# The start of a decoder-layer kernel: conditioning row by transposes, more modulation buffers, `u` ahead of the weight copies

## The chip, the cores and the metric

One core of a Trainium2 chip runs the whole program. The metric is the device time of one execution in microseconds (us). Matrix work is done by TensorE (PE), element-wise work by VectorE (DVE) and ScalarE (ACT); GpSimd (POOL) only sets constants here. SyncE (SP) issues every DMA, in program order, on one queue.

## What is computed

The reference is one residual decoder layer on 256 tokens of width 2048. Each of its two halves is modulated by a conditioning vector `c`:

```python
c_act = jax.nn.silu(c)
mod = c_act @ w_mod[l] + b_mod[l]
sh1, sc1, g1, sh2, sc2, g2 = jnp.split(mod[:, None, :], N_MOD, axis=-1)
u = x * (1.0 + sc1) + sh1
y = token_mixer(u, w_in[l], ...)
x = layer_norm(DEEPNORM_ALPHA * x + (1.0 + g1) * y, ln1_g[l], ln1_b[l])
u = x * (1.0 + sc2) + sh2
y = swiglu(u, w_gate[l], w_up[l], w_down[l])
x = layer_norm(DEEPNORM_ALPHA * x + (1.0 + g2) * y, ln2_g[l], ln2_b[l])
```

The token mixer begins with a large product `u @ w_in` whose columns feed an mLSTM group (`qk`, `v`, `o`) and an HGRN2 group (`f`, `q`, `i`, `g`). HGRN2 has a lower bound `lb` from a softmax over layers; with one layer it is zero, but the kernel still computes it.

## The kernel before

The token axis (256) lies along the free dimension, the width 2048 is cut into 16 rows of 128 partitions, called k = 0 to 15. All weights come from HBM as float32. Each 128x1024 weight tile is split into a high part (`wh`, an ACT copy to fp32r) and a low part (`wl`, a DVE subtraction, L214), and each product is three matmuls: high weight by high `u` (L250), high weight by low `u` (L251), low weight by high `u` (L252).

**Modulation.** `mod(j)` (L172) makes 128 of the 6 x 2048 modulation values: it loads a 1024 KB tile `m` of the transposed `w_mod` (L174) and DVE multiplies it with `cb` and sums along the row (L175), giving one column of `modc`. `cb` holds silu(c) in all 128 partitions. The tiles `m` have two buffers. At the start `cb` is filled by one DMA that reads the 8 KB vector `c` 128 times (L141), and two ACT passes then apply silu to it in place. A second, column-wise copy of silu(c), `ca`, is made from the packed constants `pk` (L143).

**Row k of `u`.** `make_u(k)` (L270) needs columns 16+k (scale) and k (shift) of `modc` and the transposed `x`, which comes in four loads of 512 KB (L274), one for four rows. ACT computes `u`, ACT copies it to the high part `uh`, and DVE subtracts to get the low part `ul` (L232). `prep(n)` calls `mod(16+k)`, `mod(k)` and `make_u(k)` for the rows below n.

**Order of the input product.** `STAGES` lists sections. The first is `fq`, rows 0 to 3: `fq_part` (L325) holds eight PSUM banks and for each row first runs `prep(k + 1)`, then loads two weight tiles (L209) and runs 48 matmuls on them. So every row of this section needs 2 MB of modulation weights and 1 MB of weights. After it come `qk`, `g`, `i`, `v` on rows 0 to 3 (first group), the same on rows 4 to 7 (second group), `fq` on rows 4 to 15 and the rest; the other 12 rows of `u` are prepared while these run. `evac` adds up sections; the tiles `q`, `f`, `i`, `g`, `qk`, `v` and the four halves of `uh`, `ul` take all ten buffers of the pool `big`, from which `A()` allocates.

**Order on the engines.** A scheduler orders the instructions; `tc.high_priority` raises those inside it, and the weight copies (`wh`, `wl`) have it with `PRI["w"]`. Each engine then works through its list in order: an instruction that waits holds up all behind it. `lower_bound()` (L303) is called when the first section's work is done; its first operation depends on `pk` alone. The constants `kc` (identity, two masks) and `mk` are loaded in row 3 of the first section (L330, L332).

Of the kernel before, what the change touches and what calls it, by code (L numbers as in the profile page):

```python
# [3 lines left out]
F32 = mybir.dt.float32  # L4
F32R = mybir.dt.float32r
U8 = mybir.dt.uint8
AF = mybir.ActivationFunctionType
ALU = mybir.AluOpType

P = 128  # L10
T = 256
# [69 lines left out]
def build(nc, tc, d):  # L81
    from contextlib import ExitStack

    with ExitStack() as ctx:
# [41 lines left out]
        def act(out, in_, f, **kw):  # L126
            if f in sets:
                use_set(f)
            i = nc.scalar.activation(out, in_, f, **kw).ins  # L129
            if f in sets:  # L130
                tc.add_manual_dep(i, table["load"].name, order, reason="table")
                table["used"].append(i)
            return i
# [4 lines left out]
        mm = nc.tensor.matmul  # L138

        cb = cst.tile([P, D], F32, name="cb")  # L140
        nc.sync.dma_start(cb, d["c"].broadcast_to([P, D]))  # L141
        pk = cst.tile([P, NPK], F32, name="pk")
        nc.sync.dma_start(pk, d["pk"])  # L143
        kc = cst.tile([P, NCST], F32, name="kc")
        kr = cst.tile([P, 256], F32R, name="kr")
        mk = cst.tile([P, NMK], U8, name="mk")

        def pc(n, i=0, w=1):
            return pk[:, PK[n][0] + i : PK[n][0] + i + w]
# [8 lines left out]
        one = cst.tile([P, P], F32, name="one1")  # L158
        nc.gpsimd.memset(one, 1.0)

        for i in range(2):
            o = cb[:, 1024 * i : 1024 * i + 1024]
            act(o, o, AF.Silu)
        init = cst.tile([P, 96], F32, name="init")
        nc.vector.tensor_copy(init, pc("bmod", 0, 96))
        for s in (1, 2, 4, 5):
            ts(init[:, 16 * s : 16 * s + 16], pc("bmod", 16 * s, 16), 1.0, None, ALU.add)
        ca = cst.tile([P, 16], F32, name="ca")
        act(ca, pc("c", 0, 16), AF.Silu)
        modc = cst.tile([P, 96], F32, name="modc")  # L170

        def mod(j):  # L172
            t = mr.tile([P, D], F32, tag="m", name=f"m{j}")
            nc.sync.dma_start(t, d["wmod"][j])  # L174
            table["mod"] = nc.vector.tensor_tensor_reduce(t, t, cb, 1.0, init[:, j : j + 1], ALU.mult, ALU.add, modc[:, j : j + 1]).ins  # L175
            yield
# [24 lines left out]
        def col(s, k):  # L201
            return modc[:, 16 * s + k : 16 * s + k + 1]
# [27 lines left out]
        def split(hi, lo, src):  # L230
            act(hi, src, AF.Copy)
            tt(lo, src, hi.bitcast(F32), ALU.subtract)  # L232

        def pair(n):
            return [A(F32R, name=f"{n}h{i}") for i in range(2)], [A(F32R, name=f"{n}l{i}") for i in range(2)]

        def kt(tiles, k):
            if len(tiles) > 2:
                return tiles[k]
            t = tiles[k // 8]  # L240
            return t[:, (k % 8) * T : (k % 8) * T + T]
# [21 lines left out]
                    mm(o, b, h[:, w], start=False, stop=last and k == nk - 1, skip_group_check=True)  # L263


        uh, ul = pair("u")

        xt = {}

        def make_u(k):  # L270
            u = S(T, "t", bufs=CFG["t"])
            if k % 4 == 0:
                xt["t"] = M(name="xT")
                nc.sync.dma_start(xt["t"], d["x"][k // 4])  # L274
            act(u, xt["t"][:, (k % 4) * T : (k % 4) * T + T], AF.Identity, scale=col(1, k), bias=col(0, k))
            split(kt(uh, k), kt(ul, k), u)

        acc = {"q": A(name="q"), "f": A(name="f"), "i": A(name="i"), "g": A(name="g"), "qk": A(name="qk"), "v": A(name="v")}

# [22 lines left out]

        def lower_bound():  # L303
            e, pr = lbt[:, 0:8], lbt[:, 8:16]
            tt(e, pc("lb", 0, 8), pc("lb", 0, 8), ALU.subtract)
            act(e, e, AF.Exp)
            nc.vector.reciprocal(pr, e)
            tt(pr, pr, e, ALU.mult)
            tt(lb, pr, pr, ALU.subtract)
            ts(oml, lb, -1.0, 1.0, ALU.mult, ALU.add)  # L310
# [14 lines left out]
        def fq_part(k0, k1):  # L325
            banks = [ps() for _ in range(8)]
            for k in range(k0, k1):
                prep(k + 1)
                if k == 3:
                    nc.sync.dma_start(kc, d["kc"])  # L330
                    mf = M(NMK, name="mf")
                    nc.sync.dma_start(mf, d["mk"])  # L332
                    nc.vector.tensor_copy(mk, mf)
                    act(kr[:, 0:P], ident, AF.Copy)
                    act(kr[:, P:], kc[:, 192:320], AF.Copy)
                for c, (h, l) in enumerate(next_win()):
                    gB(banks[4 * c : 4 * c + 4], h, l, 1, 1024, uh, ul, k, k == k0, k == k1 - 1)
                    yield
            if k1 == KT:
                next(ga)  # L340
            for i in range(8):
                evac(k0, "fq", i, banks[i])
# [67 lines left out]
        for st in head:  # L410
            gen = part(*st)
            unit = work([st]) / (2 * (st[3] - st[2]) if st[0] == "fq" else (st[3] - st[2]) // 2)
            for _ in gen:
                done += unit
                if done > start:
                    prep(min(KT, head[0][3] + (KT - head[0][3]) * (done - start) / (total - start)))
            if done == start:
                lower_bound()


# [640 lines left out]
def lay(x, c, w_mod, b_mod, w_in, conv_w, conv_b, b_igate, b_fgate, mlstm_norm_w, hgrn_norm_w, lb_logits, w_out, ln1_g, ln1_b, w_gate, w_up, w_down, ln2_g, ln2_b):  # L1061
# [10 lines left out]

    wm, wi, wo, wg, wu, wd = w_mod[0], w_in[0], w_out[0], w_gate[0], w_up[0], w_down[0]
    a = {}
    a["c"] = c.reshape(1, D)
    a["wmod"] = np.ascontiguousarray(wm.T).reshape(96, P, D)
    a["wmk"] = np.concatenate([wm[:, s * D : s * D + D].reshape(KT, P, D) for s in PE_SECT] or [wm[:1, :1].reshape(1, 1, 1)])
    a["x"] = x[0].T.reshape(4, 4, P, T).transpose(0, 2, 1, 3).reshape(4, P, 1024)
# [45 lines left out]
```

## Time and profile before

| what | before |
|---|---|
| median of 3 runs | 1257.38 us (1256.13 to 1259.53) |
| the profiled execution, own time | 1258.37 us |
| its span (first to last instruction) | 1256.3 us |
| PE busy | 1210.4 us, 96% of the span |
| DVE busy | 906.4 us, 72% |
| ACT busy | 595.0 us, 47% |
| DMA, 16 engines | 328 MB, mean 261 GB/s |

The profiled execution is 2.1 us longer than its span and 1.0 us longer than the median of the runs. The page shares busy time over the whole span; the first 50 us of 1256 are one slice and a half of its forty, so the change has to be read in windows and in the timeline of the first 60 us. "Matmul" rows give the time of one instruction through the pipeline; how fast PE works is the distance from one start to the next.

### The profile page before, as it was taken

The numbers are of one execution on the slowest core, as the hardware profiler recorded it, in microseconds if no ns is written. First come the engines' busy times: TensorE is split into PE (matmuls) and PEld (weight loads), VectorE is DVE, ScalarE is ACT, GpSimd is POOL, SyncE is SP. The second block draws the span as 40 slices with busy tenths as digits, with TensorE's granted clock in tenths as the row PEclk, the third lists the DMA queues.
The fourth block names the chain that finished last, engine by engine and source line by source line (L and its number), as shares of the span: only waits on it lengthen the run. The fifth ranks groups of instructions, "written<-read, shape, count | busy, mean of one in ns | idle before, by whom it ended". The sixth has DMA issues, their size and how long they took to land.

```text
span 1256.3 us, 17142 instructions
## 1 busy us (share of the span) xinstructions
PE 1210.4 (96%) x6706; PEld 1038.6 (83%) x6706; DVE 906.4 (72%) x987; ACT 595.0 (47%) x751; POOL 3.9 (0%) x13
## 2 busy tenths in 40 slices
PE   4799999999999999899999999999999999999996
PEld 4789899997889888788888888888888888888885
DVE  6688987999999867979688895555555445445665
ACT  3554445745565643664444444434344444444340
POOL 0000000000000000000000000000000000000000
PEclk9899999999999999999999999999999999999998
DMA  9998998856888896689898886566666666676661
GB/s 361 358 337 337 335 388 314 309 202 235 297 314 310 312 330 229 228 329 373 276 336 328 316 289 198 173 198 189 197 191 191 192 188 187 193 255 186 196 201 67
DMA packets 75968, 328.00 MB, mean 261 GB/s; under 512 B 8432, under 2 KB 8816, under 8 KB 62704
## 3 DMA queue, kind: packets, MB, share of 16 engines
q1 hardware_dynamic: 75888, 326.92, 74.9%
q8 instruction: 52, 0.85, 0.3%
q14 instruction: 28, 0.23, 0.0%
HBM read 324.79 MB, written 2.10 MB: 260 GB/s over the span
## 4 chain that ended last, share of the span: by engine, by line
PE 90%; DVE 4%; ACT 3%; DMA 1%; issue 1%; DVEq 0%; ACTq 0%
PE ps L726 21%; PE ps L725 21%; PE ps L729 21%; PE ps L250 5%; PE ps L252 5%; PE ps L251 5%; PE ps L261 2%; PE ps L262 2%; PE ps L263 2%; DVE m L175 1%; PE ps L448 1%; DMA m<-in_wmod 1%; ACT wh L129 1%; DVE wl L214 1%; PE ps L881 1%
## 5 line engine op out<-in xcount | busy, mean ns | idle before, releaser
L129 ACT ACTIVATE wh<-wr 128x1024 fp32r<-128x1024 f32 x405 | 427.8, 1059 | 535.4 <-PE ps L726 389.1
L719 DVE TENSOR_TENSOR wl<-wr,wh 128x1024 fp32r<-128x1024 f32 x293 | 356.5, 1223 | 258.6 <-ACT wh L129 254.2
L725 PE MATMUL ps<-wh,u2h 128*128 128x512 f32 x704 | 274.6, 391 | 3.2 <-ACT u2h L129 3.2
L726 PE MATMUL ps<-wh,u2l 128*128 128x512 f32 x704 | 274.5, 391 | 0.0
L175 DVE CUSTOM_DVE_ANT_0 m<-m,cb,init 128x2048 f32<-128x2048 f32 x96 | 225.0, 2346 | 21.5 <-DMA m<-in_wmod 21.3
L729 PE MATMUL ps<-wl,u2h 128*128 128x512 f32 x704 | 217.3, 390 | 0.0
L250 PE MATMUL ps<-uh,wh 128*128 128x256 f32 x640 | 184.9, 294 | 24.1 <-ACT wh L129 16.9
L251 PE MATMUL ps<-ul,wh 128*128 128x256 f32 x640 | 182.2, 287 | 0.0
L252 PE MATMUL ps<-uh,wl 128*128 128x256 f32 x640 | 180.5, 287 | 1.1 <-DVE wl L214 1.0
L725 PEld LDWEIGHTS ps<-wh,u2h 128*128 128x128 f32 x704 | 132.2, 188 | 31.0 <-ACT u2h L129 3.6
L726 PEld LDWEIGHTS ps<-wh,u2l 128*128 128x128 f32 x704 | 132.6, 189 | 27.9 <-DVE u2l L849 0.7
L729 PEld LDWEIGHTS ps<-wl,u2h 128*128 128x128 f32 x704 | 132.5, 188 | 27.6
L214 DVE TENSOR_TENSOR wl<-wr,wh 128x1024 fp32r<-128x1024 f32 x112 | 135.8, 1221 | 24.2 <-ACT wh L129 23.5
L250 PEld LDWEIGHTS ps<-uh,wh 128*128 128x128 f32 x640 | 124.1, 195 | 26.4 <-ACT wh L129 17.3
L725 PE MATMUL ps<-wh,hid 128*128 128x512 f32 x340 | 132.5, 390 | 0.0
L729 PE MATMUL ps<-wl,hid 128*128 128x512 f32 x340 | 132.3, 389 | 0.0
L726 PE MATMUL ps<-wh,hid 128*128 128x512 f32 x340 | 132.3, 389 | 0.0
L251 PEld LDWEIGHTS ps<-ul,wh 128*128 128x128 f32 x640 | 124.9, 195 | 1.3 <-issue 1.0
L252 PEld LDWEIGHTS ps<-uh,wl 128*128 128x128 f32 x640 | 123.5, 195 | 1.9 <-DVE wl L214 1.8
L726 PEld LDWEIGHTS ps<-wh,hid 128*128 128x128 f32 x340 | 63.8, 188 | 13.3
L729 PEld LDWEIGHTS ps<-wl,hid 128*128 128x128 f32 x340 | 63.8, 188 | 13.3
L725 PEld LDWEIGHTS ps<-wh,hid 128*128 128x128 f32 x340 | 63.8, 188 | 13.1
(191 smaller groups left out, 1049.3 us busy)
## 6 DMA issues: line engine op xcount, KB each, us to landing
m<-in_wmod SPq DMA_DIRECT2D x96, 1024.0 KB, 6.8
wr<-in_wf SPq DMA_DIRECT2D x176, 512.0 KB, 3.8
wr<-in_win SPq DMA_DIRECT2D x112, 512.0 KB, 5.9
wr<-in_wd SPq DMA_DIRECT2D x88, 512.0 KB, 3.6
wr<-in_wo SPq DMA_DIRECT2D x32, 512.0 KB, 5.3
xT<-in_x SPq DMA_DIRECT2D x4, 512.0 KB, 8.4
z<-in_xr SPq DMA_DIRECT2D x2, 1024.0 KB, 8.9
out<-z SPq DMA_DIRECT2D x8, 256.0 KB, 2.4
```

What stands on the lines that cost most here:

```text
L129: i = nc.scalar.activation(out, in_, f, **kw).ins
L175: table["mod"] = nc.vector.tensor_tensor_reduce(t, t, cb, 1.0, init[:, j : j + 1], ALU.mult, ALU.add, modc[:, j : j + 1]).ins
L214: tt(l[:, :m], r[:, :m], h[:, :m].bitcast(F32), ALU.subtract)
L250: mm(o, h[:, wsl], kt(uh, k0 + k), start=st, stop=False, skip_group_check=True)
L251: mm(o, h[:, wsl], kt(ul, k0 + k), start=False, stop=False, skip_group_check=True)
L252: mm(o, l[:, wsl], kt(uh, k0 + k), start=False, stop=en, skip_group_check=True)
L261: mm(o, a, h[:, w], start=first and k == 0, stop=False, skip_group_check=True)
L262: mm(o, a, l[:, w], start=False, stop=False, skip_group_check=True)
L719: table["low"] = tt(l, r, h.bitcast(F32), ALU.subtract).ins
L725: mm(o, a, h[:, w], start=first, stop=False, skip_group_check=True)
L726: mm(o, b, h[:, w], start=False, stop=False, skip_group_check=True)
L729: mm(o, a, l[:, w], start=False, stop=last, skip_group_check=True)
```

## The change

Five edits, in the order of the diff:

1. `cb` no longer comes by DMA. `ca` (silu of the column-wise `c` in `pk`) is computed first; PE transposes each of its 16 columns, broadcast along the free dimension, into four PSUM banks, and ACT and DVE copy two banks each to `cb`. For that the identity, 64 KB of `kc`, is loaded at the very start.
2. The modulation tiles 17, 1, 18, 2 (rows 1 and 2) get four buffers of the pool `big` of their own (`room`), beside the two of `m`. The same four buffers later hold `i`, `g`, `qk`, `v`.
3. The first load of `x` is cut into four of 128 KB, each issued in its row.
4. `make_u` has a priority above that of the weight copies.
5. `lower_bound` is called in the second group, after section `qk`, and held behind the modulation before it; the rest of `kc` and `mk` are loaded in row 5, in the second `fq` section.

```diff
--- before.py
+++ after.py
@@ -138,10 +138,10 @@
         mm = nc.tensor.matmul
 
         cb = cst.tile([P, D], F32, name="cb")
-        nc.sync.dma_start(cb, d["c"].broadcast_to([P, D]))
         pk = cst.tile([P, NPK], F32, name="pk")
         nc.sync.dma_start(pk, d["pk"])
         kc = cst.tile([P, NCST], F32, name="kc")
+        nc.sync.dma_start(kc[:, 0:128], d["kc"][:, 0:128])
         kr = cst.tile([P, 256], F32R, name="kr")
         mk = cst.tile([P, NMK], U8, name="mk")
 
@@ -158,19 +158,24 @@
         one = cst.tile([P, P], F32, name="one1")
         nc.gpsimd.memset(one, 1.0)
 
-        for i in range(2):
-            o = cb[:, 1024 * i : 1024 * i + 1024]
-            act(o, o, AF.Silu)
+        ca = cst.tile([P, 16], F32, name="ca")
+        act(ca, pc("c", 0, 16), AF.Silu)
+        for b in range(4):
+            o = ps()
+            for j in range(4):
+                nc.tensor.transpose(o[:, P * j : P * j + P], ca[:, 4 * b + j : 4 * b + j + 1].broadcast_to([P, P]), ident)
+            if b % 2:
+                nc.vector.tensor_copy(cb[:, 512 * b : 512 * b + 512], o)
+            else:
+                act(cb[:, 512 * b : 512 * b + 512], o, AF.Copy)
         init = cst.tile([P, 96], F32, name="init")
         nc.vector.tensor_copy(init, pc("bmod", 0, 96))
         for s in (1, 2, 4, 5):
             ts(init[:, 16 * s : 16 * s + 16], pc("bmod", 16 * s, 16), 1.0, None, ALU.add)
-        ca = cst.tile([P, 16], F32, name="ca")
-        act(ca, pc("c", 0, 16), AF.Silu)
         modc = cst.tile([P, 96], F32, name="modc")
 
         def mod(j):
-            t = mr.tile([P, D], F32, tag="m", name=f"m{j}")
+            t = room.pop(j) if j in room else mr.tile([P, D], F32, tag="m", name=f"m{j}")
             nc.sync.dma_start(t, d["wmod"][j])
             table["mod"] = nc.vector.tensor_tensor_reduce(t, t, cb, 1.0, init[:, j : j + 1], ALU.mult, ALU.add, modc[:, j : j + 1]).ins
             yield
@@ -263,6 +268,7 @@
                     mm(o, b, h[:, w], start=False, stop=last and k == nk - 1, skip_group_check=True)
 
 
+        room = {j: A(name="room") for j in (17, 1, 18, 2)}
         uh, ul = pair("u")
 
         xt = {}
@@ -271,9 +277,14 @@
             u = S(T, "t", bufs=CFG["t"])
             if k % 4 == 0:
                 xt["t"] = M(name="xT")
-                nc.sync.dma_start(xt["t"], d["x"][k // 4])
-            act(u, xt["t"][:, (k % 4) * T : (k % 4) * T + T], AF.Identity, scale=col(1, k), bias=col(0, k))
-            split(kt(uh, k), kt(ul, k), u)
+                if k:
+                    nc.sync.dma_start(xt["t"], d["x"][k // 4])
+            if k < 4:
+                w = slice(k * T, k * T + T)
+                nc.sync.dma_start(xt["t"][:, w], d["x"][0][:, w])
+            with tc.high_priority(PRI["w"] + 400):
+                act(u, xt["t"][:, (k % 4) * T : (k % 4) * T + T], AF.Identity, scale=col(1, k), bias=col(0, k))
+                split(kt(uh, k), kt(ul, k), u)
 
         acc = {"q": A(name="q"), "f": A(name="f"), "i": A(name="i"), "g": A(name="g"), "qk": A(name="qk"), "v": A(name="v")}
 
@@ -302,7 +313,8 @@
 
         def lower_bound():
             e, pr = lbt[:, 0:8], lbt[:, 8:16]
-            tt(e, pc("lb", 0, 8), pc("lb", 0, 8), ALU.subtract)
+            i = tt(e, pc("lb", 0, 8), pc("lb", 0, 8), ALU.subtract).ins
+            tc.add_manual_dep(i, table["mod"].name, order, reason="late")
             act(e, e, AF.Exp)
             nc.vector.reciprocal(pr, e)
             tt(pr, pr, e, ALU.mult)
@@ -326,8 +338,8 @@
             banks = [ps() for _ in range(8)]
             for k in range(k0, k1):
                 prep(k + 1)
-                if k == 3:
-                    nc.sync.dma_start(kc, d["kc"])
+                if k == 5:
+                    nc.sync.dma_start(kc[:, 128:], d["kc"][:, 128:])
                     mf = M(NMK, name="mf")
                     nc.sync.dma_start(mf, d["mk"])
                     nc.vector.tensor_copy(mk, mf)
@@ -414,7 +426,7 @@
                 done += unit
                 if done > start:
                     prep(min(KT, head[0][3] + (KT - head[0][3]) * (done - start) / (total - start)))
-            if done == start:
+            if st[0] == "qk" and st[2] == 4 and st[1] == 1:
                 lower_bound()
 
 
@@ -1072,7 +1084,6 @@
 
     wm, wi, wo, wg, wu, wd = w_mod[0], w_in[0], w_out[0], w_gate[0], w_up[0], w_down[0]
     a = {}
-    a["c"] = c.reshape(1, D)
     a["wmod"] = np.ascontiguousarray(wm.T).reshape(96, P, D)
     a["wmk"] = np.concatenate([wm[:, s * D : s * D + D].reshape(KT, P, D) for s in PE_SECT] or [wm[:1, :1].reshape(1, 1, 1)])
     a["x"] = x[0].T.reshape(4, 4, P, T).transpose(0, 2, 1, 3).reshape(4, P, 1024)
```

What this does to the order is read at three places. First SP, the list of DMAs from the start (`cb`, `pk`, `kc`, `xT` as above; `m16` is the modulation tile of column 16, `room5` to `room8` are columns 17, 1, 18, 2; `wr` are weight tiles). Before:

```order
L141 DMA cb_82<-in_c 128x2048
L143 DMA pk_84<-in_pk 128x242
L174 DMA m16_128<-in_wmod 128x2048
L174 DMA m0_131<-in_wmod 128x2048
L274 DMA xT21_135<-in_x 128x1024
L209 DMA wr22_140<-in_win 128x1024
L209 DMA wr23_170<-in_win 128x1024
L174 DMA m17_200<-in_wmod 128x2048
L174 DMA m1_203<-in_wmod 128x2048
L209 DMA wr25_210<-in_win 128x1024
L209 DMA wr26_240<-in_win 128x1024
```

SP in the changed kernel (its lines are those of the changed file):

```order
L144 DMA kc_85<-in_kc 128x128
L179 DMA m16_154<-in_wmod 128x2048
L179 DMA m0_157<-in_wmod 128x2048
L284 DMA xT29_161<-in_x 128x256
L214 DMA wr30_166<-in_win 128x1024
L214 DMA wr31_196<-in_win 128x1024
L284 DMA xT29_161<-in_x 128x256
L214 DMA wr33_235<-in_win 128x1024
L214 DMA wr34_265<-in_win 128x1024
L179 DMA room5_131<-in_wmod 128x2048
L179 DMA room6_132<-in_wmod 128x2048
L179 DMA room7_133<-in_wmod 128x2048
```

`cb` is gone (`pk` is now the first), row 1's weight tiles have moved ahead of its modulation tiles, and the modulation of row 2 follows that of row 1 without row 2's weights between them.

Second DVE, from its start to the low part of row 0's weights. Before (`lbt` is the lower bound, ISA is the multiply-and-sum of L175 and the read of its sum):

```order
L165 COPY init_100<-pk_84 128x96
L305 TENSOR_TENSOR lbt11_119<-pk_84 128x8
L167 TENSOR_SCALAR init_100<-pk_84 128x16 x4
L307 RECIPROCAL lbt11_119<-lbt11_119 128x8
L175 ISA m16_128,modc_108<-m16_128,cb_82,init_100 128x2048
L175 ISA modc_108 128x1
L308 TENSOR_TENSOR lbt11_119<-lbt11_119 128x8
L309 TENSOR_TENSOR lbt11_119<-lbt11_119 128x8
L310 TENSOR_SCALAR lbt11_119<-lbt11_119 128x8
L175 ISA m0_131,modc_108<-m0_131,cb_82,init_100 128x2048
L175 ISA modc_108 128x1
L232 TENSOR_TENSOR ul03_111<-t20_134,uh01_109 128x256
```

DVE in the changed kernel:

```order
L172 COPY init_124<-pk_83 128x96
L174 TENSOR_SCALAR init_124<-pk_83 128x16 x4
L168 COPY cb_82<-ps2_106 128x512
L168 COPY cb_82<-ps4_118 128x512
L180 ISA m16_154,modc_130<-m16_154,cb_82,init_124 128x2048
L180 ISA modc_130 128x1
L180 ISA m0_157,modc_130<-m0_157,cb_82,init_124 128x2048
L180 ISA modc_130 128x1
L219 TENSOR_TENSOR wl30_169<-wr30_166,wh30_168 128x1024
L237 TENSOR_TENSOR ul011_137<-t28_160,uh09_135 128x256
```

The lower bound has left this place, two copies of `cb` have come, and `wl30` stands ahead of row 0's `ul`.

Third DVE a little later, around row 1 of `u`. Before:

```order
L214 TENSOR_TENSOR wl23_173<-wr23_170,wh23_172 128x1024
L175 ISA m17_200,modc_108<-m17_200,cb_82,init_100 128x2048
L175 ISA modc_108 128x1
L175 ISA m1_203,modc_108<-m1_203,cb_82,init_100 128x2048
L175 ISA modc_108 128x1
L214 TENSOR_TENSOR wl25_213<-wr25_210,wh25_212 128x1024
L232 TENSOR_TENSOR ul03_111<-t24_206,uh01_109 128x256
```

The changed kernel:

```order
L219 TENSOR_TENSOR wl31_199<-wr31_196,wh31_198 128x1024
L219 TENSOR_TENSOR wl33_238<-wr33_235,wh33_237 128x1024
L219 TENSOR_TENSOR wl34_268<-wr34_265,wh34_267 128x1024
L180 ISA room5_131,modc_130<-room5_131,cb_82,init_124 128x2048
L180 ISA modc_130 128x1
L180 ISA room6_132,modc_130<-room6_132,cb_82,init_124 128x2048
L180 ISA modc_130 128x1
L180 ISA room7_133,modc_130<-room7_133,cb_82,init_124 128x2048
L180 ISA modc_130 128x1
L237 TENSOR_TENSOR ul011_137<-t32_230,uh09_135 128x256
```

Row 1's weight copies `wl33`, `wl34` now stand ahead of its modulation, and one modulation of row 2 (`room7`) stands between the modulation and the `ul` of row 1.

## Rows read from the trace of the kernel before

**Rows 1.** The page, part 1: busy time of each engine.

```profile
PE 1210.4 (96%) x6706; PEld 1038.6 (83%) x6706; DVE 906.4 (72%) x987; ACT 595.0 (47%) x751; POOL 3.9 (0%) x13
```

**Rows 2.** Timeline, PE: start, duration, instruction, in brackets idle time before and releaser.

```profile
16.65 0.58 PE L250 MATMUL ps<-uh,wh 128*128 128x256 f32 x1 [16.65 <-ACT wh L129]
...
33.56 0.63 PE L250 MATMUL ps<-uh,wh 128*128 128x256 f32 x3 [2.43 <-ACT uh L129]
...
44.38 1.75 PE L250 MATMUL ps<-uh,wh 128*128 128x256 f32 x6 [4.71 <-ACT uh L129]
```

**Rows 3.** Windows: stretch, length, busy PE PEld DVE ACT POOL, PEclk, DMA share, GB/s.

```profile
16.65:22.40 5.75, 5.75 (x26) 5.63 (x27) 5.75 (x5) 1.56 (x2) 0.00 (x0) 1.00 1.03 392
22.40:31.00 8.60, 8.60 (x72) 8.52 (x71) 7.12 (x8) 2.37 (x4) 0.00 (x0) 1.00 0.93 363
...
44.00:50.00 6.00, 5.62 (x26) 5.61 (x27) 5.95 (x5) 4.01 (x7) 0.18 (x1) 0.51 1.02 397
```

**Rows 4.** Windows again: the rest of the input product.

```profile
50.00:200.00 150.00, 147.28 (x1043) 137.88 (x1043) 128.06 (x128) 75.38 (x97) 1.48 (x2) 1.00 0.93 352
```

**Rows 5.** Timeline of ACT and of DVE up to row 0.

```profile
5.64 2.00 ACT L129 ACTIVATE cb<-cb 128x1024 f32<-128x1024 f32 x2 [3.63 <-DMA cb<-in_c]
7.76 1.28 ACT L121 ACT_TABLE_LOAD   x1
9.06 0.21 ACT L129 ACTIVATE lbt<-lbt 128x8 f32<-128x8 f32 x1
9.30 0.20 DVE L307 RECIPROCAL lbt<-lbt 128x8 f32<-128x8 f32 x1 [2.56 <-ACT lbt L129]
9.46 2.35 DVE L175 CUSTOM_DVE_ANT_0 m<-m,cb,init 128x2048 f32<-128x2048 f32 x1
12.22 2.34 DVE L175 CUSTOM_DVE_ANT_0 m<-m,cb,init 128x2048 f32<-128x2048 f32 x1
14.61 0.60 ACT L129 ACTIVATE t<-xT,modc 128x256 f32<-128x256 f32 x1 [4.04 <-DVE modc L175]
15.24 0.42 ACT L129 ACTIVATE uh<-t 128x256 fp32r<-128x256 f32 x1
15.56 1.99 ACT L129 ACTIVATE wh<-wr 128x1024 fp32r<-128x1024 f32 x2
```

**Rows 6.** One tile, `m`, issues at 1.64 us: time to landing.

```profile
L174 SPq DMA_DIRECT2D m<-in_wmod x1: 424/424/424, 1.6 to 1.6; - x1
...
DMA to landing us min/median/max: 7.5/7.5/7.5
```

**Rows 7.** The same for the issue at 2.1 us.

```profile
L174 SPq DMA_DIRECT2D m<-in_wmod x1: 532/532/532, 2.1 to 2.1; - x1
...
DMA to landing us min/median/max: 9.5/9.5/9.5
```

**Rows 8.** Chain of waits up to 46 us: start, duration, what.

```profile
0.73 4.88 DMA cb<-in_c
...
32.45 7.49 DMA m<-in_wmod
40.08 2.35 DVE m L175
```

**Rows 9.** Waits of SP's queue, 0 to 44 us: total, times, longest.

```profile
SPq L174 <- DVE modc L175: 19.1, 6, 5.3
```

**Rows 10.** Windows: DMA where the queue was fed, and where it waited.

```profile
10.00:20.00 10.00, 3.35 (x14) 3.23 (x15) 8.30 (x11) 3.48 (x5) 0.00 (x0) 1.00 1.01 416
20.00:40.00 20.00, 17.25 (x131) 16.79 (x130) 16.07 (x16) 6.05 (x8) 0.00 (x0) 1.00 0.95 354
```

**Rows 11.** Timeline, PE: transposes of the same form, later in the program.

```profile
415.00 1.91 PE L704 MATMUL ps<-kc,modc 128*128 128x128 f32 x16
```

**Rows 12.** Groups by form, DVE, 0 to 140 us: busy, mean ns, idle before.

```profile
L214 DVE TENSOR_TENSOR wl<-wr,wh 128x1024 fp32r<-128x1024 f32 x38 | 46.0, 1222 | 17.3 <-ACT wh L129 17.2
L232 DVE TENSOR_TENSOR ul<-t,uh 128x256 fp32r<-128x256 f32 x10 | 4.2, 421 | 1.1 <-ACT uh L129 1.1
...
L291 DVE TENSOR_TENSOR qk<-ps,qk 128x512 f32<-128x512 f32 x4 | 2.7, 687 | 0.3 <-PE ps L252 0.3
```

**Rows 13.** Timeline, DVE: two reductions one behind the other.

```profile
18.91 2.35 DVE L175 CUSTOM_DVE_ANT_0 m<-m,cb,init 128x2048 f32<-128x2048 f32 x1
...
21.18 2.35 DVE L175 CUSTOM_DVE_ANT_0 m<-m,cb,init 128x2048 f32<-128x2048 f32 x1
```

## The prediction

> **What bounds the kernel now.** First the page: PE is busy 96% of the span [rows 1]. An edit can therefore gain little over the program as a whole, and what matters is where PE's missing 4% lies. The timeline of PE gives a good half of it in three pauses: 16.65 us before the first matmul, 2.43 us ahead of the third row of `u`, 4.71 us ahead of the fourth [rows 2], 23.8 us in all before 44 us. The windows show a second loss there. From 22.4 to 31 us 72 matmuls take 8.60 us, 0.119 us each; from 16.65 to 22.4 us, after the long pause, 26 take 5.75 us, 0.221 each, and from 44 to 50 us, after the pause of 4.71, again 26, at a granted clock of 0.51 (the 1.2 GHz level; the first stretch is shown as 1.00, but its pace is that of the low level) [rows 3]. Each such stretch costs 5.75 - 26 x 0.119 = 2.65 us. The pause of 2.43 us cost no clock: 131 matmuls fit into 17.25 busy us from 20 to 40 us [rows 10].
>
> Afterwards PE is the bound: from 50 to 200 us it is busy 147.28 of 150 us [rows 4]. The fourth row's 48 matmuls (26 by 50.0 us, 22 more at 0.119) are through at 52.6 us. What is gained by then is kept if DMA and DVE, busy 0.93 and 128.06 of 150 us there, keep their lead.
>
> What do the pauses wait for? The timeline of ACT and DVE up to row 0 [rows 5]: `cb` lands, two silu passes, a table load, `exp` of the lower bound, DVE's RECIPROCAL at 9.30 behind it, and only then the first reduction at 9.46, the second at 12.22, `t` and `uh` at 14.61 and 15.24, and last the weight copy at 15.56. But the data are hardly earlier: the first `m` lands at 1.64 + 7.5 = 9.1 us [rows 6], the second at 2.1 + 9.5 = 11.6 [rows 7]. For rows 2 and 3 the chain of waits names the DMA: the last `m` is issued at 32.45, lands at 39.94, its reduction starts at 40.08 [rows 8]. SP had waited 19.1 us for a free buffer of `m` [rows 9]. While the queue was fed it moved 416 GB/s (10 to 20 us), in the stretch with those waits 354 (20 to 40 us) [rows 10]. So the start is bound by the DMA queue, and DVE stands close behind.
>
> **Edit 1, `cb` by transposes.** 1.05 MB of DMA go, 2.52 us at 416 GB/s; 64 KB of identity, 0.16 us, come. `m16` lands at 9.1 - 2.4 = 6.7, `m0` at 9.25. The new path to `cb` has no row. Its parts: `cb`'s DMA took 4.88 us [rows 8], 2.36 more than its bytes; so `pk` (124 KB, 0.3 us), now first, lands at 0.73 + 2.36 + 0.3 = 3.4, the identity at about 3.7. Silu of `ca` takes about 0.2. Sixteen transposes take 1.91 us later in the program [rows 11]; PE is cold here, so 1.91 x 0.221/0.119 = 3.5. The last copy from PSUM is at most the 0.69 us of an addition of that shape [rows 12]. `cb` is complete at 3.75 + 3.5 + 0.7 = 7.95 us. With the warm pace it would be 6.3; were each of the four banks to wait for a copy of its own, 9 us. I take 7.9, nearest to the cold matmuls that follow.
>
> **Edit 5, lower bound.** At the front nothing of it waits any more. In its new place it costs six DVE operations of 0.2 us at most, one `exp` of 0.21 and a table load of 1.28 on ACT [rows 5], beside a PE that has work; bounds 0 and 2.7 us. I take 0.6, since ACT is idle half of that stretch (75.38 of 150 us busy) and DVE a seventh [rows 4]. The table load is followed by an ACTIVATE at 9.06, 0.02 us after its end at 9.04 [rows 5]. The Trainium skill (ScalarE: Activation LUTs, What ACT_TABLE_LOAD costs) counts a drain with each switch, 2.66 us in all; by that figure this term would be up to 1.4 us larger, an estimate. The trace shows no such drain, and its row is used.
>
> **Edits 1 and 4, row 0.** The reductions start 2.27 us apart [rows 13]: 7.9 and 10.2, the second done at 12.6. `x` (128 KB, landed 9.6) and the first weights (10.8) are there, and the weight copy is now ahead of `t`; then 1.1 us for `t` and `uh` as before. PE starts at 13.75 instead of 16.65. Row 0 takes 5.75 + 22 x 0.119 = 8.4 us, till 22.1.
>
> **Edits 2 and 3, rows 1 to 3.** With the buffers free, the queue stays fed. At 416 GB/s from `m0` at 9.25 the order of the list gives: row 1's weights 14.9, `m17` and `m1` 17.45 and 19.95, `m18` and `m2` 22.5 and 25.0, row 2's weights 27.8, `m19` and `m3` 30.4 and 32.9 (before 39.94), row 3's weights 35.7. Now DVE is late next. Behind `m0` it has `wl30`, `ul`, `wl31`, `wl33`, `wl34` (1.2 and 0.4 us each [rows 12], and 0.6 of waiting for `wh31`): done at 18.2, then `m17` and `m1` until 22.7. `u` of row 1 is ready at 23.8: PE pauses 1.7 us. Its eight high matmuls run, but `ul` stands behind `m18` (25.0) and comes at 25.35: 0.65 more. Row 1 ends at 30.2. `m2` at 27.65 and `u` at 28.75 are in time, row 2 runs till 36.0. `wl36`, `ul`, `wl37` bring DVE to 30.9, `m19` and `m3` to 35.5, `u` of row 3 comes at 36.6: a pause of 0.65. All three pauses are below the 2.43 us that kept the clock, so row 3 runs warm and ends at 42.5. Before it was 52.6: **10.1 us earlier**.
>
> **Afterwards.** The order of the weights is unchanged, but the DMA lead is thinner: the queue reaches the weights behind row 3 about 7.5 us earlier, PE 10 us earlier. At 416 GB/s the third tile of `qk` lands at 44.5, its `wl` is done at about 47.7, and PE wants it at 48.1. I take 0.5 us for this, between 0 and the whole 2.5.
>
> **The sum.** -10.1 + 0.6 + 0.5 = -9.0 us against the profiled execution's own 1258.37 us (span 1256.3 and 2.1 around it): 1249.4. That execution stood 1.0 us above the median, so I predict 1257.38 - 9.0 = 1248.4, rounded to **1248.5**.
>
> **Rivals.**
> - *The queue is not faster with more buffers.* For: even with SP's waits the engines were 0.95 busy [rows 10], so the 354 GB/s may be what mixed traffic gives. From 9.25 us the 9.85 MB up to `m3` take 27.8 us: 37.1, reduction 39.4, `u` 40.5, row 3 ends at 46.4. That is 6.2 earlier, less 0.6: about 1252. Against: 416 over ten fed microseconds. Chance 0.15.
> - *One pause too long.* If the transposes, a late `wh31` or a late `m17` make the pause before row 1 or row 3 more than 2.43 and up to 4.71 us, one row falls to 0.221 a matmul: 2.65 us more, 1251. Chance 0.08.
> - *The gain is lost later.* DVE and DMA at 85% and 0.93 up to 200 us [rows 4] may not follow 10 us earlier; then only the DMA's share, 2.4 to 7 us, is kept: 1251 to 1255. Against: no reordered instruction there, and SP's list in that stretch differs by two small loads alone. Chance 0.08.
> - *Each small transfer costs its fixed part.* If the three additional transfers ahead of row 3 (net) each held up the queue for the 2.36 us that `cb` took beyond its bytes, 7.1 us are given back: 1255.5. Against: fed, with half-megabyte tiles among the large ones, the queue made 416 GB/s, which leaves no such gaps. Chance 0.03. The Trainium skill (DMA: Bandwidth & Descriptors, Rules for kernel authors) asks for 1 MiB and more per DMA and for small transfers to be joined, which edit 3 undoes; the fed stretch of this trace does not bear out a loss at 512 KB, and 128 KB no row here shows.
> - *Slower.* The short pauses that now follow each row keep PE at the low level all through the section: 192 matmuls at 0.221 are 42.5 us, from 13.75 till 56.2, 3.6 later than now, with the 1.1 of the other terms 1262. It decides whether a pause of 0.65 to 1.7 us lowers the clock, or undoes what the row before had done to raise it; the one of 2.43 us did not. Chance 0.03.
> - *It does nothing:* the transfers set the end as before, and the saved megabyte is eaten by the new path to `cb`. 1257. Chance 0.01, since 2.5 us of traffic are certainly gone.
>
> **How the numbers follow.** The forecast has the remaining 0.62; its own bounds are a gain of 7 to 11.5 us (`cb` at 6.3 or 9, lower bound 0 to 2.7, the lead). A measurement of this kernel can tell 0.3%, 3.8 us, from no change. Faster by more: 0.62 + 0.15 + 0.08 and half of the third rival, 0.88 rounded down; within: the other half, the fourth and the last, 0.09; slower 0.03. The range: from 1245.5 (a gain of nearly 12) to 1253.5, which takes in the first two rivals and part of the third.
>
> **What would show it.** In the changed profile: first reduction near 7.9 us and first matmul near 13.7; no wait of SP for `modc` up to row 3, and over 400 GB/s from 10 to 33 us; the last modulation of the section landed near 33; PE pauses of 1 to 2 us ahead of row 1 and below 1 us ahead of row 3, at a granted clock that stays up from about 20 us; the 192nd matmul near 42.5; from there to 200 us PE idle by not much more than the 2.72 us of before. A fourth row at half clock, or SP waiting again, would make it wrong by 2.5 to 4 us; a busy share of PE from 45 to 200 us clearly below 98% would mean that the gain is not kept.

## The result and the profile after

| what | before | changed |
|---|---|---|
| median of the runs beside each other | 1257.58 us (4 runs, 1256.13 to 1259.53) | 1251.58 us (4 runs, 1250.02 to 1251.91) |
| ratio, 95% interval | | 0.9949 [0.9935, 0.9963] |
| the profiled execution, own time | 1258.37 us | 1251.47 us |
| its span | 1256.3 us | 1249.6 us |

The change saves 6.0 us in the medians and 6.9 us between the two profiled executions. A second set of five runs of the changed kernel on another occasion gave 0.9956 [0.9942, 0.9971]. The forecast was 9.0 us, in a range that holds 1251.58.

The timeline of PE in the changed kernel (start, duration, instruction; in brackets the idle time before it and what ended it) shows the pauses; it answers to [rows 2]:

```profile
3.27 3.44 PE L166 MATMUL ps<-kc,ca 128*128 128x128 f32 x16 [3.27 <-DMA kc<-in_kc]
13.44 1.01 PE L255 MATMUL ps<-uh,wh 128*128 128x256 f32 x3 [6.73 <-ACT uh L129]
...
24.07 2.07 PE L255 MATMUL ps<-uh,wh 128*128 128x256 f32 x8 [3.21 <-ACT uh L129]
```

The sixteen transposes take 3.44 us at 3.27, where 3.5 at 3.75 was forecast. The first matmul is at 13.44 instead of 16.65. The pause ahead of row 2 is gone, and the 4.71 us ahead of row 3 as well (PE reaches row 3 at 38.58 without a pause), but a new one of 3.21 us stands ahead of row 1.

The windows (length, busy time of PE, PEld, DVE, ACT, POOL, then granted clock, DMA share, GB/s) answer to [rows 10] and [rows 4]:

```profile
10.00:20.00 10.00, 6.56 (x43) 6.56 (x44) 9.23 (x8) 5.02 (x6) 0.00 (x0) 0.67 1.03 421
20.00:40.00 20.00, 16.79 (x116) 16.41 (x115) 17.66 (x19) 7.71 (x11) 0.74 (x1) 0.83 1.02 413
...
50.00:200.00 150.00, 147.40 (x1045) 138.01 (x1044) 128.93 (x133) 75.60 (x96) 2.23 (x3) 1.00 0.94 356
```

The queue now moves 413 GB/s from 20 to 40 us, before 354. Up to 44 us SP's waits for a free buffer (total, times, longest) have fallen from 19.1 us to 8.0. All three stand ahead of modulation tiles of later rows, issued at 34.34, 36.89 and 43.84 us:

```profile
SPq L179 <- DVE modc L180: 8.0, 3, 4.4
```

Finer windows of the same columns show the clock. It is at the low level until row 0 is about half through, rises by 17 us, is lost again for 24 to 30 us, behind the new pause, and returns:

```profile
13.40:15.00 1.60, 1.56 (x7) 1.56 (x8) 1.27 (x3) 1.60 (x2) 0.00 (x0) 0.50 1.05 428
...
17.00:18.00 1.00, 1.00 (x11) 1.00 (x10) 0.90 (x1) 0.00 (x0) 0.00 (x0) 1.00 1.04 434
...
24.00:26.00 2.00, 1.94 (x9) 1.94 (x10) 2.00 (x4) 0.01 (x1) 0.00 (x0) 0.50 1.00 388
...
28.00:30.00 2.00, 2.00 (x11) 2.00 (x11) 1.60 (x4) 1.97 (x4) 0.00 (x0) 0.50 1.03 422
...
31.00:33.00 2.00, 2.00 (x19) 2.00 (x18) 1.48 (x2) 0.00 (x0) 0.00 (x0) 1.00 1.00 396
```

The timeline of DVE (reductions) and then of ACT show what row 3 waits for:

```profile
7.59 2.35 DVE L180 CUSTOM_DVE_ANT_0 m<-m,cb,init 128x2048 f32<-128x2048 f32 x1
...
9.86 2.35 DVE L180 CUSTOM_DVE_ANT_0 m<-m,cb,init 128x2048 f32<-128x2048 f32 x1
...
34.51 2.35 DVE L180 CUSTOM_DVE_ANT_0 m<-m,cb,init 128x2048 f32<-128x2048 f32 x1 [0.19 <-DMA m<-in_wmod]
```

```profile
36.19 1.06 ACT L129 ACTIVATE wh<-wr 128x1024 fp32r<-128x1024 f32 x1 [6.01 <-DMA wr<-in_win]
37.16 0.59 ACT L129 ACTIVATE t<-xT,modc 128x256 f32<-128x256 f32 x1
37.78 0.42 ACT L129 ACTIVATE uh<-t 128x256 fp32r<-128x256 f32 x1
...
47.48 0.60 ACT L129 ACTIVATE qk<-ps 128x512 f32<-128x512 f32 x1 [1.80 <-PE ps L257]
```

The reductions of row 0 begin at 7.59 and 9.86 (forecast 7.9 and 10.2). The last reduction of the section starts at 34.51, as soon as its tile has landed, where the forecast has 33.2 (35.5 less 2.35); the first weight copy of row 3 starts at 36.19, also when its tile has landed, and stands ahead of `t` in ACT's list. So `uh` of row 3 is ready at 38.2 instead of 36.6.

The end of the first section is hard to see in these rows. The first eviction of section `qk` (a copy out of PSUM) follows it by about 3.2 us and serves as a mark. It comes at 47.48; before it came at 55.78 (timeline of ACT of the kernel before):

```profile
55.78 0.60 ACT L129 ACTIVATE qk<-ps 128x512 f32<-128x512 f32 x1 [1.57 <-PE ps L252]
```

That is 8.3 us earlier. Two later groups of matmuls, named by source line, show what becomes of this lead: the gates' and mLSTM's mask matmuls (minimum, median and maximum ns, then first to last start). Before:

```profile
L376 PE MATMUL gps<-ul,wgh x16: 276/278/284, 216.1 to 221.4; 128*36 128x256 f32 x16
```

```profile
L543 PE MATMUL ps<-kr x4: 327/328/328, 341.2 to 355.5; 128*128 128x128 f32 x4
```

Changed:

```profile
L388 PE MATMUL gps<-ul,wgh x16: 276/278/284, 207.6 to 212.9; 128*36 128x256 f32 x16
```

```profile
L555 PE MATMUL ps<-kr x4: 327/327/328, 334.3 to 348.6; 128*128 128x128 f32 x4
```

At 216 us the lead is 8.5 us, at 341 us 6.9; between them 1.6 us are lost. The loss lies behind one place, where PE has a pause of 3.10 us in both kernels, waiting for DVE. At its end the lead is still 8.5 us (timeline of PE, before and changed):

```profile
314.62 1.13 PE L495 MATMUL ps<-q,kk 128*128 128x128 f32 x8 [3.10 <-DVE q L479]
```

```profile
306.09 1.46 PE L507 MATMUL ps<-q,kk 128*128 128x128 f32 x8 [3.10 <-DVE q L491]
```

Behind it the clock stayed up before, and fell in the changed kernel (windows behind the pause, before and changed):

```profile
314.00:316.00 2.00, 1.38 (x10) 1.37 (x11) 2.00 (x4) 0.21 (x1) 0.00 (x0) 1.00 0.92 375
316.00:318.00 2.00, 2.00 (x10) 1.62 (x10) 2.00 (x3) 0.44 (x2) 0.00 (x0) 1.00 0.94 377
```

```profile
306.00:308.00 2.00, 1.91 (x10) 1.84 (x11) 2.00 (x3) 0.41 (x2) 0.00 (x0) 0.68 0.95 385
308.00:310.00 2.00, 2.00 (x6) 1.52 (x6) 2.00 (x4) 0.25 (x1) 0.00 (x0) 0.50 0.81 324
```

The change edits nothing at that place.

### The profile page after: what moved, and what is told of

It is laid out like the page before. It is cut to its first block, busy times and chain, and to the rows that moved or that the text cites. A ratio compares the mean times of both kernels' runs of the same rounds, so it can differ in the third digit from the quotient of the medians.

```text
span 1249.6 us, 17176 instructions
## 1 busy us (share of the span) xinstructions
PE 1214.4 (97%) x6722; PEld 1041.9 (83%) x6722; DVE 908.4 (73%) x989; ACT 594.0 (48%) x751; POOL 3.9 (0%) x13
## 4 chain that ended last, share of the span: by engine, by line
PE 91%; DVE 4%; ACT 2%; DMA 1%; issue 1%; SPq 0%; DVEq 0%; ACTq 0%
PE ps L738 22%; PE ps L741 21%; PE ps L737 21%; PE ps L255 5%; PE ps L257 5%; PE ps L256 5%; PE ps L266 2%; PE ps L267 2%; PE ps L268 2%; PE ps L460 1%; DVE wl L219 1%; DMA room<-in_wmod 1%; PE ps L893 1%; ACT wh L129 1%; DVE m L180 1%
## 5 line engine op out<-in xcount | busy, mean ns | idle before, releaser
L180 DVE CUSTOM_DVE_ANT_0 m<-m,cb,init 128x2048 f32<-128x2048 f32 x92 | 215.7, 2347 | 13.9 <-DMA m<-in_wmod 13.4
L255 PE MATMUL ps<-uh,wh 128*128 128x256 f32 x640 | 184.1, 293 | 10.2 <-ACT uh L129 9.9
```

Of the source, the lines that this page charges most:

```text
L255: mm(o, h[:, wsl], kt(uh, k0 + k), start=st, stop=False, skip_group_check=True)
```

## The experiments

**Theory A** is that of the forecast: the section's end is set by the queue, through the landing of the fourth row's modulation and weights. **Theory B**: the path to `cb` at the start is what mattered. **Theory C**: the clock lost in row 1 is what the forecast lacked. **Theory D**, formed from the profiles of the first four runs: a pause lowers the clock in some executions and not in others, and that takes part of the gain and makes the spread. The mark is the first `qk` eviction as above; before 55.78, changed 47.48. Differences in time are between medians unless said otherwise; each run was timed beside runs of the kernel before.

**Edit 1 alone** (`a1_cb`), the kernel before with

```diff
-        nc.sync.dma_start(cb, d["c"].broadcast_to([P, D]))
+        nc.sync.dma_start(kc[:, 0:128], d["kc"][:, 0:128])
...
-            act(o, o, AF.Silu)
+                nc.tensor.transpose(o[:, P * j : P * j + P], ca[...].broadcast_to([P, P]), ident)
```

> The kernel before with edit 1 alone (cb by transposes, identity loaded first). Theory A (the section's end is set by when the queue delivers the fourth row's modulation, and by the pace of the queue): only the saved megabyte counts, 2.4 us; SP still waits about 19 us for modc, the fourth row's u comes near 41.5 us and its matmuls still run at the low level; the 192nd matmul near 50, time 2.4 us below before (ratio 0.998). Theory B (the path to cb at the start is what mattered): most of the 6 to 7 us appear already here, 192nd matmul below 47.

Measured: 1256.84 against 1257.32, ratio 0.9996 [0.9986, 1.0006]: no difference that can be told. In its profile the first reduction is at 7.89 and the mark at 51.86, 3.9 us earlier than in the profile of before. Timeline of PE (rows 2 and 3) and the window from 20 to 40 us:

```profile
32.12 1.01 PE L255 MATMUL ps<-uh,wh 128*128 128x256 f32 x3 [3.48 <-ACT uh L129]
...
40.91 0.74 PE L255 MATMUL ps<-uh,wh 128*128 128x256 f32 x4 [1.41 <-ACT uh L129]
```

```profile
20.00:40.00 20.00, 15.68 (x116) 15.07 (x114) 16.58 (x17) 7.25 (x11) 0.70 (x2) 0.91 1.00 371
```

SP waits 25.4 us for `modc`, more than before, and the queue makes 371 GB/s. B falls: it asked for an end of the section below 47, a mark below 50.2. A's direction is right, and the profile's mark moves by more than its 2.4 us; but the medians do not show even these (upper bound of the gain 1.8). Part of the profile's lead is lost near 306 us (table below); where the rest goes is open.

**Edit 2 alone** (`a2_room`), the kernel before with

```diff
+            t = room.pop(j) if j in room else mr.tile([P, D], F32, tag="m", name=f"m{j}")
...
+        room = {j: A(name="room") for j in (17, 1, 18, 2)}
```

> The kernel before with edit 2 alone (the modulation of rows 1 and 2 gets four buffers of its own). Theory A: the queue is fed (SP waits under 10 us for modc up to 44 us, 20 to 40 us over 400 GB/s), the pause ahead of the fourth row shrinks, the first qk eviction comes 5.5 to 7 us earlier than the 55.78 of before, time 3 to 5 us below before. Rival (the edits work only together): under 1.5 us.

Measured: 1255.43 against 1257.56, ratio 0.9982 [0.9973, 0.9991], 2.1 us faster. SP waits 4.0 us for `modc`, the queue is fed, and the pause ahead of the fourth row is 2.62 us (window from 20 to 40 us, timeline of PE):

```profile
20.00:40.00 20.00, 17.15 (x132) 16.52 (x130) 18.41 (x19) 6.93 (x11) 1.01 (x2) 1.00 1.02 414
```

```profile
40.60 0.74 PE L250 MATMUL ps<-uh,wh 128*128 128x256 f32 x4 [2.62 <-ACT uh L129]
```

The mark comes at 51.73, 4.05 us earlier. Mark and time both move by less than A expected (5.5 to 7 us and 3 to 5 us). One reason is that the clock fell behind this pause too (0.56 and 0.59 from 42 to 46 us); whether it is the whole reason is open.

**The change without edit 1** (`u1_cbdma`): the diff of `a1_cb` the other way round, in the changed kernel.

> The changed kernel with edit 1 undone (cb again by the 1 MB DMA, identity with the rest of kc in row 5). Theory A: all landings 2.4 us later, queue still fed at over 400 GB/s, 192nd matmul near 46.8 instead of 44.4, time 3.5 to 4.5 us below before. Theory B: the gain is gone, 0 to 1 us below before.

Measured: 1253.74 against 1257.32, ratio 0.9968 [0.9955, 0.9981]: 3.6 us faster than before in the medians, 4.0 by the ratio, as A says; mark 49.06, 1.6 us behind the changed kernel's. The window from 20 to 40 us shows the fed queue:

```profile
20.00:40.00 20.00, 17.24 (x125) 16.73 (x125) 18.11 (x17) 6.12 (x10) 0.61 (x1) 0.91 1.02 415
```

**The change without edit 2** (`u2_noroom`):

```diff
-        room = {j: A(name="room") for j in (17, 1, 18, 2)}
+        room = {}
```

> The changed kernel with edit 2 undone (two modulation buffers only). Theory A: SP waits for modc again (15 to 20 us up to row 3), 20 to 40 us at about 355 GB/s, the fourth row behind a pause of 4 to 5 us and at the low level, 192nd matmul near 49.5, time 2.5 to 3.5 us below before. Rival (queue pace does not hang on the buffers): within 1 us of the changed kernel.

Measured: 1258.02 against 1257.32, ratio 1.0009 [0.9997, 1.0021]: in the medians the whole gain is gone. SP waits 28.0 us for `modc`. Windows, the fourth row in the timeline of PE, and the mark in that of ACT:

```profile
10.00:20.00 10.00, 6.46 (x38) 6.46 (x39) 8.38 (x10) 3.02 (x4) 0.00 (x0) 0.66 0.99 366
20.00:40.00 20.00, 15.34 (x108) 14.40 (x106) 15.71 (x15) 5.83 (x8) 0.00 (x0) 0.91 0.99 360
```

```profile
42.08 1.22 PE L255 MATMUL ps<-uh,wh 128*128 128x256 f32 x4 [3.52 <-ACT uh L129]
```

```profile
52.30 0.60 ACT L129 ACTIVATE qk<-ps 128x512 f32<-128x512 f32 x1 [1.57 <-PE ps L257]
```

That edit 2 carries the change is shown: without it the time is some 6 us longer, far beyond the intervals. The queue makes only 366 GB/s already from 10 to 20 us, where before had 416. A reading of this, not tried by itself: `m17` cannot be issued before the first reduction ends, at about 10.05 us, and without `cb` and three quarters of the first `x` the queue holds 1.4 MB less to bridge that. The 2.5 to 3.5 us that A left to the other edits did not appear in the medians. In the profile they did: the mark is 3.5 us earlier than before, and this execution, at 1256.06 us one of the faster of its ten runs, is 2.3 us shorter than the profiled one of before.

Together, in the medians: edit 1 alone is worth 0.5 us, edit 2 alone 2.1, the whole 6.0; without edit 1 3.6 remain, without edit 2 nothing. So edit 2 is what the gain cannot do without, and the whole is more than the two edits by themselves. Whether the saved megabyte is worth more where the queue is kept full is not shown: it gives 0.5 us alone and about 2.4 on top of the rest, but with intervals that overlap, and at the mark it is the other way round (3.9 alone, 1.6 on top).

**The pause ahead of row 1 filled** (`w1_zero`), with `zr` a tile of zeros (its making is left out here), so that the sums are unchanged:

```diff
...
+                    if k == 0 and c == 1:
+                        for n in range(24):
+                            mm(banks[7][:, T:], zr, kt(uh, 0), start=False, stop=False, skip_group_check=True)
```

> The changed kernel with 24 matmuls of zero weights added behind row 0's 48, into one of its banks (they add nothing to the sums), so that PE has no pause of 3.2 us ahead of row 1. Theory A (row 3's u, ready at 38.2, sets the end whatever row 1 does): row 1 runs at the high level and ends 2.6 us earlier, but a pause ahead of row 3 takes its place; 192nd matmul at 43.9 to 44.4, time within 0.5 us of the changed kernel. Theory C (the lost clock of row 1 is what the forecast lacked): 192nd matmul near 41.8, time 2.5 us below the changed kernel.

Measured: 1251.97, ratio to before 0.9955 [0.9941, 0.997], no faster than the changed kernel. In the profile the clock stays at 1.00 from 20 us on, and a pause ahead of row 3 takes the place of the slow row 1 (timeline of PE):

```profile
25.90 0.39 PE L260 MATMUL ps<-ul,wh 128*128 128x256 f32 x1 [0.52 <-DVE ul L241]
...
37.77 0.62 PE L259 MATMUL ps<-uh,wh 128*128 128x256 f32 x3 [1.06 <-ACT uh L129]
```

The mark is at 47.00, 0.5 us earlier. A holds for the section, C falls: of the 2.6 us that row 1 loses at half clock all but some 0.5 were waiting time anyway. But this profiled execution took 1249.54 us, 1.9 less than the changed kernel's, and its gain of 9.0 us at the gates is still 9.0 at mLSTM: there the clock had stayed up behind the pause of 3.10 us. That led to D.

**That pause filled as well** (`w2_zero`, in addition to the edit of `w1_zero`):

```diff
...
+            if hf == 1:
+                for n in range(25):
+                    mm(o[:, :T], zr, kr, start=True, stop=True, skip_group_check=True)
```

> The run w1_zero with 25 more matmuls of zero weights, in the pause of 3.1 us that PE has near 306 us ahead of the last block product of the second half of HGRN2. Theory D (that pause lowers the clock in some executions and not in others, 1.5 us each time): the clock stays at 1.00 there in the profile, median 0.5 to 1.5 us below w1_zero's 1251.97. Rival (the pause costs nothing by the clock): median as w1_zero's, or up to 1 us above by the added matmuls.

Measured: 1250.05 (1248.95 to 1252.59) against 1257.56, ratio 0.9946 [0.9934, 0.9959]. Where PE paused, it is busy throughout, at full clock:

```profile
302.00:310.00 8.00, 8.00 (x51) 7.23 (x52) 7.96 (x9) 2.35 (x5) 0.00 (x0) 1.00 0.94 352
```

The lead at the gates, 6.6 us, is kept (6.9 at mLSTM). But in this execution the clock fell at another place, behind a pause of only 1.79 us ahead of row 3 (timeline of PE, and a window behind it):

```profile
38.66 0.62 PE L259 MATMUL ps<-uh,wh 128*128 128x256 f32 x3 [1.79 <-ACT uh L129]
```

```profile
41.00:46.00 5.00, 5.00 (x33) 5.00 (x33) 3.22 (x3) 3.23 (x6) 0.00 (x0) 0.70 1.02 416
```

So the mark is at 49.39, 2.4 behind `w1_zero`'s. The profiles agree with D; the medians of the two runs, 1.9 us apart, have intervals that overlap.

**Edit 3 undone, and half of edit 5** (`u3_x`: one load of 512 KB for the first `x`; `u5_lb`: the lower bound called when the first section's work is done, without the hold behind the modulation; the loads of `kc` and `mk` stay in row 5):

```diff
-                if k:
-                    nc.sync.dma_start(xt["t"], d["x"][k // 4])
-            if k < 4:
-                w = slice(k * T, k * T + T)
-                nc.sync.dma_start(xt["t"][:, w], d["x"][0][:, w])
+                nc.sync.dma_start(xt["t"], d["x"][k // 4])
```

> The changed kernel with the first x load whole again (512 KB ahead of row 0's weights). Theory A: row 0's weights land 0.9 us later, row 0 starts up to 0.9 us later, but by the fourth row the queue has moved the same bytes: first qk eviction within 0.5 us of 47.48, time within 1 us of the changed kernel. Rival (each small transfer costs the queue its fixed part): first qk eviction 2 us or more earlier.

```diff
-            i = tt(e, pc("lb", 0, 8), pc("lb", 0, 8), ALU.subtract).ins
-            tc.add_manual_dep(i, table["mod"].name, order, reason="late")
+            tt(e, pc("lb", 0, 8), pc("lb", 0, 8), ALU.subtract)
...
-            if st[0] == "qk" and st[2] == 4 and st[1] == 1:
+            if done == start:
                 lower_bound()
```

> The changed kernel with the lower bound made at the front again. Theory A: its exp and table load delay cb by 1 to 2 us at most, first reduction 7.6 to 9.5 us, first qk eviction within 1 us of 47.48 since the queue sets the fourth row; time within 1 us of the changed kernel. Rival (the lower bound at the front was a wait that mattered): 1.5 to 3 us slower than the changed kernel.

Measured: 0.9956 [0.9943, 0.997] and 0.9961 [0.9946, 0.9976], marks at 47.72 and 47.98. Neither edit's worth can be told from nothing. Without the split the first matmul is at 15.34 instead of 13.44, and yet the section ends only 0.24 us later: by then the queue has moved the same bytes. The Trainium skill (DMA: Bandwidth & Descriptors, Rules for kernel authors) asks for many small transfers to be joined into one large one. For 128 KB pieces in a full queue no run here shows a loss or a gain of time. With the lower bound at the front the first reduction is at 7.88.

The other half of edit 5, the later loads of `kc` and `mk`, was not tried by itself. Nor was edit 4. But without edit 4 SP's list is the same, and so are the first 50 rows of ACT's list and the first 54 of DVE's, which reach beyond the first section; only behind them do some `uh` and `ul` change places with neighbours. So edit 4 orders nothing in the first section.

**All pauses over 1.1 us filled** (`w3_zero`: 26 zero matmuls behind row 0, 10 behind row 2, 25 as in `w2_zero`), beside the changed kernel once more (`after_again`). The difference to `w2_zero`:

```diff
-                    if k == 0 and c == 1:
-                        for n in range(24):
-                            mm(banks[7][:, T:], zr, kt(uh, 0), start=False, stop=False, skip_group_check=True)
+                    if k in (0, 2) and k0 == 0 and c == 1:
+                        for n in range(26 if k == 0 else 10):
+                            mm(banks[7][:, T:], zr, kt(uh, k), start=False, stop=False, skip_group_check=True)
```

> The run w2_zero with 26 zero matmuls behind row 0 and 10 more behind row 2, so that no pause over 1.1 us is left in the first section or at the 3.1 us place. Theory D (pauses lower the clock in some executions only, and that, beside the later landing, took the rest of the forecast gain): clock 1.00 in the profile from 20 to 50 us and near 306 us, first qk eviction near 47.0, time 1 to 2 us below the changed kernel run beside it and a narrower spread. Rival (the clock's lapses cost nothing the section's end feels): within 0.5 us of the changed kernel.

> The changed kernel unchanged, beside w3_zero on the same chip. All theories: 5 to 7 us below before. Theory D: in this execution's profile the pauses of about 3 us ahead of row 1 and near 306 us may or may not lower the clock; the spread of its runs is 2 to 3 us or more.

Measured: `w3_zero` 1250.42 (four of its five runs from 1249.83 to 1250.65, one 1252.58), ratio 0.9943 [0.993, 0.9955]; `after_again` 1251.59 (1251.00 to 1254.34), 0.9956 [0.9942, 0.9971]. The profile of `w3_zero` shows a clock of 1.00 from 14 to 48 us and near 306 us (up to 18 us, though, PE's pace is that of the low level, 5 to 7 matmuls in a microsecond instead of 10 or 11), and pauses of 0.36 and 0.64. Timeline of PE, and the mark in that of ACT:

```profile
26.13 0.39 PE L260 MATMUL ps<-ul,wh 128*128 128x256 f32 x1 [0.36 <-DVE ul L241]
...
39.10 0.74 PE L259 MATMUL ps<-uh,wh 128*128 128x256 f32 x4 [0.64 <-ACT uh L129]
```

```profile
48.21 0.60 ACT L129 ACTIVATE qk<-ps 128x512 f32<-128x512 f32 x1 [1.57 <-PE ps L261]
```

In `after_again` the clock fell behind both pauses, 3.12 us ahead of row 1 and 3.10 near 303 us, and yet its mark, at 47.27, is 0.9 us earlier than `w3_zero`'s, which was expected near 47.0. So in the first section the filled pauses gained nothing; from 20 to 40 us the queue of `w3_zero` made 392 GB/s, that of `after_again` 411. The difference in time, 1.2 us, is of the size that D gives for the pause near 306 us, but the intervals overlap: that the filled kernel beats the changed one is not shown. Nor is the narrower spread that was expected, 2.75 us between fastest and slowest run against 3.34.

**All profiles side by side.** The lead is the start of the gates' and of mLSTM's mask matmuls against the profile of before (216.1 and 341.2 us); between the two lies the pause of 3.10 us.

| profile | mark, us | lead at the gates | lead at mLSTM | clock behind the pause of 3.10 us | gain in the medians |
|---|---|---|---|---|---|
| changed | 47.48 | 8.5 | 6.9 | fell | 6.0 |
| `after_again` | 47.27 | 8.7 | 7.1 | fell | 6.1 |
| `a1_cb` | 51.86 | 3.9 | 2.3 | fell | 0.5 |
| `a2_room` | 51.73 | 4.0 | 2.4 | fell | 2.1 |
| `u1_cbdma` | 49.06 | 6.9 | 5.5 | fell | 3.6 |
| `u2_noroom` | 52.30 | 3.6 | 2.1 | fell | -0.7 |
| `u5_lb` | 47.98 | 8.0 | 6.5 | fell | 4.8 |
| `u3_x` | 47.72 | 8.3 | 8.3 | stayed up | 5.2 |
| `w1_zero` | 47.00 | 9.0 | 9.0 | stayed up | 5.4 |
| `w2_zero` | 49.39 | 6.6 | 6.9 | no pause | 7.5 |
| `w3_zero` | 48.21 | 7.8 | 8.1 | no pause | 7.3 |

In the profile of before the clock stayed up. In every profile where it fell, 1.4 to 1.6 us of the lead are gone at mLSTM; in the two others with the pause nothing is lost. This bears D out for that place, as far as kernels with the same code there can be compared. That executions of one and the same kernel differ too is seen in the 51 runs of before that were timed beside these: in 29 the mean granted clock was 0.993, and they took 1256.8 us on average; in 14 it was 0.992 (1258.4 us), in eight 0.990 or 0.991 (1259.2 us). At which pauses those eight lost their clock the mean does not tell.

## Why the prediction was right, and where it was too large

- *What bounds the start*: right. Edit 2 feeds the queue (354 to 413 GB/s) and carries the change, as `u2_noroom` shows; the first rival (no faster queue) did not come.
- *Edit 1 and row 0*: right to 0.3 us (7.59, 9.86, 13.44 against 7.9, 10.2, 13.7). By itself (`a1_cb`) it moves the mark by 3.9 us, and the medians do not show it.
- *Row 1*: the pause was forecast as 1.7 us and was 3.21. Row 0 ran at the low level for some 3 us, not 5.75, so it ended at 20.9 instead of 22.1, and `uh` came at 24.0. The clock then fell, which is the second rival. Only some 0.5 us of its price of 2.65 was paid, as `w1_zero` shows: row 3's `u` was hardly there earlier. That a rival came and cost little was luck.
- **The step that failed** is the end of the first section, "10.1 us earlier": it was 8.3. The landing times were laid one behind another at 416 GB/s. The queue's rate was as forecast (window from `m0`'s landing to `m3`'s):

```profile
9.25:34.50 25.25, 17.85 (x112) 17.64 (x113) 22.90 (x23) 8.96 (x12) 0.00 (x0) 0.73 1.02 415
```

At 415 GB/s these 25.25 us make 10.5 MB, but the list up to `m3` has 9.85 MB, 390 GB/s. The other 0.6 MB went to transfers issued behind `m3`: the last `x` (issued at 20.56, landed at 34.9) and row 3's weights (issued at 23.11 and 25.6, landed at 36.1 and 37.3) took a share before `m3` was complete. So the last reduction started 1.3 us late, and the weight copy that stands ahead of `t` held it 0.3 us more, until 37.16.

- *Afterwards, +0.6 and +0.5*: neither was there. The lead of 8.3 us was 8.5 at the gates, and `u5_lb` is no faster than the change. PE was busy 147.40 of 150 us from 50 to 200 us, before 147.28.
- *Not in the sum*: the pause of 3.10 us near 306 us, 1.6 us dearer in the changed kernel's profile than in that of before, which happened to keep its clock there; the prediction counted on the rest of the program running as in that one profile.
- *The balance*: 9.0 forecast, 1.8 less at the section's end, 1.1 more for the two terms that were not there, 1.6 less near 306 us make 6.7; measured are 6.9 between the profiled executions, and 6.0 between the medians, since the profiled execution of before stood 0.8 above its median. The way and the cause were forecast; the gain was put half as large again as it is, and the range holds the result because it had room for two rivals.
- The second rival's premise, that a pause of 2.43 us keeps the clock, was one case taken for a threshold.

## What to carry to other kernels

Where the first rows are bound by one DMA queue, look first for what makes the queue wait: here four buffers that let it run ahead were worth more than a megabyte of saved traffic (taken out of the changed kernel, some 6 us against 2.4). When landing times are laid one behind the other, leave a few per cent for transfers that are issued later and take a share, here 415 against 390 GB/s. And filling a pause of TensorE gains little where the next transfer sets the end anyway.

## What was not expected of the hardware

The same pause, of the same length and in the same code, lowers the clock in one profile and not in another. The pause of 3.10 us on DVE near 306 us is in ten profiles here: in seven the granted clock fell to 0.50 behind it, for some 3.4 us, in three it did not (before, `w1_zero`, `u3_x`). These are nine kernels; the one that was profiled twice, the changed one, lost its clock both times. In the first section pauses of 1.41, 1.79, 2.11, 2.24, 2.62 and 2.65 us were followed by a fall, those of 1.98 and 2.43 were not; none up to 1.08 was, all from 3.12 on were. Length is not all that differs: behind those of 1.41 and 2.62 us stood a second one of 0.21, behind that of 2.24 one of 0.52, and no run sets the two apart.

A fall near 306 us costs 1.4 to 1.6 us, in a kernel whose runs spread over 6 us (1254.97 to 1260.89 in 27 runs of before). A single profile therefore shows one draw, and a difference of 1 to 3 us between two profiles should not be put down to an edit until the clock's row has been read in both.
